# A mixture of experts written as one line of steps, with a fixed order on three engines and four pairs of split weights

## The chip, the cores and the metric

The kernel runs on one core of a Trainium2 chip. The metric is the device time of one execution in microseconds (us), the median of several. PE is TensorE, ACT is ScalarE, DVE is VectorE, POOL is GpSimd and SP is SyncE, whose queue issues most of the DMAs.

## The reference

One decoder layer in float32 on 1024 tokens of width 1024. Its last part, a mixture of experts, is what the change touches: each token goes to one of four groups and there to two of eight experts of inner width 512.

```python
x = x + parallel_mixer(rms_norm(x))          # window attention | spatial gating
x = x + memory_cross_attention(rms_norm(x))
# mixture of experts, for every token t and its two experts e:
hid = silu(x_t @ w1[e]) * (x_t @ w3[e])      # 1024 -> 512
y_t += gate[t, e] * (hid @ w2[e])            # 512 -> 1024
```

The experts' weights are 32 x 3 matrices of 1024 x 512 in float32, 2 MB each.

## The kernel before

The layer runs in stages: token mixer, memory attention, then the mixture of experts, which the change concerns. In it the program keeps 32 lists of up to 96 tokens (`cap`, `n`), one list for each expert, in the tile `idx`, and the experts are taken in a fixed line (`order`). For one expert the work is:

- GpSimd gathers its 96 rows from DRAM into X0 or X1 (L1027, two buffers in turn). TensorE transposes them in eight 128-wide pieces (L1044), and ScalarE and VectorE split the result into a high half xh and a remainder xl (L107, L108).
- SyncE brings the expert's weights as twelve tiles `ew` of 128 x 1024 (512 KB) into a ring of 36 tiles (`nraw` 19 and `nmore` 17). ScalarE casts each tile into `hi` (L1054), VectorE subtracts to get `lo` (L1055). A pair hi, lo lives in one of three pairs of buffers (`nhl` 3), and is released by the last of the six matmuls that read it. These six are two times the three products hi*xh, lo*xh and hi*xl (L115, L116, L117). The text calls such a group of a tile a step: eight steps go up, into two accumulators `h` of 96 x 512, and four go down, into two accumulators `y`.
- Between up and down lie silu on ScalarE (L1073), a product on VectorE (L1074, tile `g`), four transposes (L1081) and their split (hh, hlo).
- ScalarE multiplies y with the gate into the tile B (L1098, two instructions), and GpSimd adds B to the output in DRAM (L1033, "scatter"). B has one buffer.

`Moe.main` writes this expert by expert, with the down steps of the expert before behind the up steps of this one. Within that, the order of the instructions on each engine is chosen by the scheduler that builds the program. `rest` is the second half of the routing, with the gates of half of the tokens: twelve small products on GpSimd fill two tiles `vg` (L982, one buffer), four matmuls read each (L985), VectorE adds to `tb`, which holds the gates. `between` runs it after the first four up steps of expert 0. `counts` (L1159 to L1172) are eight matmuls, and on VectorE some twenty small instructions on 128 x 32 elements that depend on one another; they decide on a loop for lists that overflow, and stand at expert 20.

Of the kernel before, what the change touches and what calls it, by code (L numbers as in the profile page):

```python
# [17 lines left out]
P = 128  # L18
# [810 lines left out]
class Moe:  # L829
# [4 lines left out]
    def __init__(self, tc, a, L, m, cap):  # L834
        self.tc, self.nc, self.a, self.L, self.m = tc, tc.nc, a, L, m
        self.cap = cap

# [43 lines left out]
    def route(self, hf):  # L881
# [95 lines left out]
        n = 0  # L977
        for e in range(2):
            vg = w.tile([P, 2, 3, 4, NE], BF16, name="vg")
            for k in range(3):  # L980
                for i, x in enumerate((rb[:, k, e], rb[:, k, 2])):
                    G.tensor_tensor(vg[:, i, k], E[:, e], bc(x, NE), op=ALU.mult)  # L982
# [53 lines left out]

    def columns(self, x, n):
        nc, L, m = self.nc, self.L, self.m
        xh = L["ew"].tile([P, 8, self.cap], R32, name="xh", bufs=1)
        xl = L["ew"].tile([P, 8, self.cap], R32, name="xl", bufs=1)  # L1040
        for h in range(2):
            pt = L["ps"].tile([P, 4, P], F32, name="tp", bufs=2)
            for k in range(4):
                nc.tensor.transpose(pt[:, k, :n], x[:n, (4 * h + k) * P:(4 * h + k + 1) * P], m.ident[:n, :n])  # L1044
            s = slice(4 * h, 4 * h + 4)
            m.split(xh[:, s, :n], xl[:, s, :n], pt[:, :, :n])
        return xh, xl

    def parts(self, w):

        L, nc = self.L, self.nc
        hi = L["hl"].tile([P, 1024], R32, name="hi", bufs=self.nhl)
        lo = L["hl"].tile([P, 1024], R32, name="lo", bufs=self.nhl)
        nc.scalar.copy(hi, w)  # L1054
        nc.vector.tensor_sub(lo, w, hi.bitcast(F32))  # L1055
        return hi, lo

    def hidden(self, w, xc, rs, n, between=lambda: None):
# [3 lines left out]
        for i in range(2):  # L1062
            if i:
                between()
            p = L["ps"].tile([P, 512], F32, name="h", bufs=4)
            for u in range(4):
                wh, wl = self.parts(w[i][u])
                for j in range(2):
                    k, s = 2 * u + j, slice(j * 512, (j + 1) * 512)
                    m.mm3(p[:n], xh[:, k, :n], xl[:, k, :n], wh[:, s], wl[:, s], k == 0, k == 7)  # L1070
            ps.append(p)
        g = L["ew"].tile([P, 512], F32, name="g", bufs=1)
        nc.scalar.activation(g[:n], ps[0][:n], AF.Silu, scale=rs[:n])  # L1073
        nc.vector.scalar_tensor_tensor(g[:n], ps[1][:n], rs[:n], g[:n], op0=ALU.mult, op1=ALU.mult)  # L1074
        return g

    def turn(self, g, n):
        nc, L, m = self.nc, self.L, self.m
        pt = L["ps"].tile([P, 4, P], F32, name="tp", bufs=2)
        for k in range(4):  # L1080
            nc.tensor.transpose(pt[:, k, :n], g[:n, k * P:(k + 1) * P], m.ident[:n, :n])  # L1081
        hh = L["ew"].tile([P, 4, self.cap], R32, name="hh", bufs=1)
        hl = L["ew"].tile([P, 4, self.cap], R32, name="hlo", bufs=1)
        m.split(hh[:, :, :n], hl[:, :, :n], pt[:, :, :n])
        return hh, hl

    def output(self, w, hc, b, gate, n):
        nc, L, m = self.nc, self.L, self.m
        hh, hl = hc
        py = [L["ps"].tile([P, 512], F32, name="y", bufs=2) for _ in range(2)]  # L1090
        for k in range(4):
            wh, wl = self.parts(w[2][k])
            for h in range(2):
                s = slice(h * 512, (h + 1) * 512)
                m.mm3(py[h][:n], hh[:, k, :n], hl[:, k, :n], wh[:, s], wl[:, s], k == 0, k == 3)
        for h in range(2):
            s = slice(h * 512, (h + 1) * 512)
            nc.scalar.activation(b[:n, s], py[h][:n], AF.Copy, scale=gate[:n])  # L1098
# [4 lines left out]
    def main(self, xd, out, pre, rest):  # L1103
# [13 lines left out]
        X, B = (lambda i: self.X[i % len(self.X)]), (lambda i: self.B[i % len(self.B)])  # L1117
        get = lambda i: self.gather(X(i)[:n], ix(i), xd)
        for i in range(len(self.X)):
            get(i)  # L1120
        xc = self.columns(X(0), n)
        prev = None
        turned = []

        def between():
            run_all(rest)
            if prev:
                turned.append(self.turn(prev[3], n))

        def finish():  # L1130
            i, e, w, g = prev
            b = B(i)
            self.output(w, turned.pop() if turned else self.turn(g, n), b, tb[:, 0, e:e + 1], n)
            ordered(self.scatter(b[:n], ix(i), out), i)

        for i in range(NE):
            if i == 20:
                self.counts()
            e = order[i]
            w = pre.pop(e) if e in pre else self.expert(e)  # L1140
            if i + len(self.X) < NE:
                get(i + len(self.X))
            with self.tc.issue_after(self.ready.ins) if i == 0 else nullcontext():
                g = self.hidden(w, xc, tb[:, 1, e:e + 1], n, between)
            if i + 1 < NE:
                xc = self.columns(X(i + 1), n)
            if prev:
                finish()
# [279 lines left out]
```

## Time and profile before

| what | value |
|---|---|
| median of three runs | 1301.59 us (1296.95 to 1305.77) |
| the profiled execution | 1294.25 us |
| its span, first to last instruction | 1292.5 us |
| PE busy | 1225.0 us, 95% of the span |
| DVE busy | 983.0 us, 76% |
| ACT busy | 851.8 us, 66% |
| POOL busy | 195.1 us, 15% |

The span leaves 1.75 us of the profiled execution outside. That execution is 7.34 us below the median of the three, which themselves lie 8.82 us apart. Time is counted from the start of the span. The expert stage begins at 689.06 us with the first matmul of expert 0 and lasts to the end.

### The profile page before, as it was taken

The page shows a single profiled execution, that of the slowest core. Times are in us where ns is not written, and L with a number is a line of the kernel's source. Part 1 is how long each engine was busy: PE and PEld are TensorE (multiplying, and loading weights), DVE is VectorE, ACT ScalarE, POOL GpSimd, SP SyncE. Part 2 cuts the span into 40 slices and gives each one's busy share as a digit, 9 for nine tenths or more (in the row PEclk, how much of TensorE's full clock was granted, in tenths as well). Part 3 has the DMA queues.
Part 4 walks back from the last instruction along what each step waited for, and adds up shares of the span by engine and source line. Part 5 has one row for each costly group of instructions (what it writes and reads, how often), then busy time and mean ns, then how long its engine had stood idle before and what let it go on. Part 6 is the DMA issues. An engine that isn't in the chain of part 4 may idle for free.

```text
span 1292.5 us, 17753 instructions
## 1 busy us (share of the span) xinstructions
PE 1225.0 (95%) x5967; PEld 925.7 (72%) x5967; DVE 983.0 (76%) x1587; ACT 851.8 (66%) x1335; POOL 195.1 (15%) x229
## 2 busy tenths in 40 slices
PE   8999889999999999999978999999999999999995
PEld 6886668887887777888754777777777767666663
DVE  6558896556376998546567999999999999888884
ACT  6458663445357764445334888888888888877773
POOL 1311320011211113010013111111111111111000
PEclk9999899998999999999989999999999999999998
DMA  8527566345333346632799989999999999999921
GB/s 290 157 75 232 185 164 206 114 123 183 119 106 114 115 146 188 189 92 87 250 356 352 348 289 384 360 383 380 389 379 380 383 376 383 369 379 360 378 55 15
DMA packets 116190, 317.81 MB, mean 246 GB/s; under 512 B 13824, under 2 KB 35456, under 8 KB 116096
## 3 DMA queue, kind: packets, MB, share of 16 engines
q1 hardware_dynamic: 95280, 283.04, 60.5%
q0 software_dynamic: 12224, 29.38, 9.2%
q10 hardware_dynamic: 8592, 4.23, 1.1%
q8 instruction: 48, 0.79, 0.3%
q14 instruction: 46, 0.38, 0.1%
HBM read 293.52 MB, written 31.46 MB: 251 GB/s over the span
## 4 chain that ended last, share of the span: by engine, by line
issue 40%; PE 32%; DVE 8%; DMA 7%; POOL 7%; ACT 3%; POOLq 0%; SPq 0%; DVEq 0%; ACTq 0%
PE mm L115 7%; PE mm L117 7%; PE mm L116 7%; POOL out_dram L1033 3%; POOL X L1027 2%; DMA out_dram<-st 2%; DVE wlo L100 2%; DMA raw<-in_wp_dram 2%; DVE S L498 1%; PE sc L115 1%; DMA ew<-in_wm_dram 1%; PE sc L116 1%; PE sc L117 1%; DVE S L481 1%; ACT whi L99 1%
## 5 line engine op out<-in xcount | busy, mean ns | idle before, releaser
L1055 DVE TENSOR_TENSOR lo<-ew,hi 128x1024 fp32r<-128x1024 f32 x384 | 457.6, 1220 | 65.6 <-ACT hi L1054 55.4
L1054 ACT CAST hi<-ew 128x1024 fp32r<-128x1024 f32 x384 | 398.0, 1050 | 84.6 <-PE h L117 54.8
L116 PE MATMUL h<-lo,xh 128*96 128x512 f32 x512 | 204.8, 400 | 5.9 <-DVE lo L1055 5.9
L115 PE MATMUL h<-hi,xh 128*96 128x512 f32 x512 | 201.2, 395 | 3.4 <-ACT hi L1054 2.6
L117 PE MATMUL h<-hi,xl 128*96 128x512 f32 x512 | 202.1, 395 | 0.3 <-DVE xl L108 0.3
L115 PE MATMUL mm<-ah,whi 128*128 128x512 f32 x416 | 165.3, 399 | 4.4 <-ACT whi L99 2.6
L117 PE MATMUL mm<-ah,wlo 128*128 128x512 f32 x416 | 163.2, 393 | 1.5 <-DVE wlo L100 1.5
L99 ACT CAST whi<-raw 128x1024 fp32r<-128x1024 f32 x92 | 96.2, 1049 | 103.7 <-PE mm L116 56.5
L116 PE MATMUL mm<-al,whi 128*128 128x512 f32 x416 | 163.5, 393 | 0.0
L100 DVE TENSOR_TENSOR wlo<-raw,whi 128x1024 fp32r<-128x1024 f32 x92 | 112.0, 1224 | 54.8 <-ACT whi L99 54.8
L116 PEld LDWEIGHTS h<-lo,xh 128*96 128x96 f32 x512 | 82.7, 161 | 45.5 <-DVE lo L1055 10.2
L115 PEld LDWEIGHTS h<-hi,xh 128*96 128x96 f32 x512 | 82.6, 161 | 41.5 <-ACT hi L1054 5.6
L117 PEld LDWEIGHTS h<-hi,xl 128*96 128x96 f32 x512 | 82.7, 161 | 33.4 <-DVE xl L108 1.2
L116 PE MATMUL y<-lo,hh 128*96 128x512 f32 x256 | 102.2, 399 | 0.1
L117 PE MATMUL y<-hi,hlo 128*96 128x512 f32 x256 | 100.6, 393 | 0.0
L115 PE MATMUL y<-hi,hh 128*96 128x512 f32 x256 | 96.3, 400 | 0.9 <-ACT hh L107 0.9
L115 PE MATMUL mm<-whi,ah 128*128 128x512 f32 (+1 forms) x256 | 95.0, 371 | 0.2 <-DVE kn L280 0.2
L116 PE MATMUL mm<-wlo,ah 128*128 128x512 f32 (+1 forms) x256 | 93.6, 366 | 0.8 <-DVE wlo L100 0.8
L117 PE MATMUL mm<-whi,al 128*128 128x512 f32 (+1 forms) x256 | 93.6, 366 | 0.0
L115 PEld LDWEIGHTS mm<-ah,whi 128*128 128x128 f32 x416 | 78.3, 189 | 20.5 <-ACT whi L99 3.5
L117 PEld LDWEIGHTS mm<-ah,wlo 128*128 128x128 f32 x416 | 78.3, 188 | 19.0 <-DVE wlo L100 3.0
L116 PEld LDWEIGHTS mm<-al,whi 128*128 128x128 f32 x416 | 78.4, 188 | 15.3 <-DVE al L111 0.5
(318 smaller groups left out, 1976.6 us busy)
## 6 DMA issues: line engine op xcount, KB each, us to landing
ew<-in_wm_dram SPq DMA_DIRECT2D x384, 512.0 KB
raw<-in_wp_dram SPq DMA_DIRECT2D x92, 512.0 KB
xr<-in_xT_dram SPq DMA_DIRECT2D x24, 256.0 KB
xr<-in_x_dram SPq DMA_DIRECT2D x16, 256.0 KB
km<-md POOLq DMA_DIRECT2D x8, 512.0 KB, 4.5
x1d<-q SPq DMA_DIRECT2D x16, 256.0 KB
xr<-x1d SPq DMA_DIRECT2D x16, 256.0 KB
sq<-in_xT_dram SPq DMA_DIRECT2D x8, 256.0 KB
```

What stands on the lines that cost most here:

```text
L99: nc.scalar.copy(hi, w)
L100: nc.vector.tensor_sub(lo, w, hi.bitcast(F32))
L115: mm(out, ah, bh, start=start, stop=False)
L116: mm(out, ah, bl, start=False, stop=False)
L117: mm(out, al, bh, start=False, stop=stop)
L481: nc.vector.tensor_tensor_reduce(out=S[:, j, kc], in0=ps[:, i, kc], in1=self.mask[:, kc], scale=1.0, scalar=-3.0e38, op0=ALU.add, op1=ALU. ...
L498: nc.vector.tensor_scalar(S[:, j, kc], S[:, j, kc], st[:, 5, j:j + 1], None, op0=ALU.mult)
L1027: return self.nc.gpsimd.indirect_dma_start(out=x, out_offset=None, in_=src, in_offset=bass.IndirectOffsetOnAxis(ap=idx, axis=0), bounds_ch ...
L1033: return self.nc.gpsimd.indirect_dma_start(out=dst, out_offset=bass.IndirectOffsetOnAxis(ap=idx, axis=0), in_=x, in_offset=None, bounds_ch ...
L1054: nc.scalar.copy(hi, w)
L1055: nc.vector.tensor_sub(lo, w, hi.bitcast(F32))
```

## The change

The expert stage becomes one list of steps (eight up steps of expert i, four down steps of expert i-1, and so on). Every instruction of ScalarE, VectorE and TensorE for the experts is pinned to the order in which it is written (`self.pin`). A step's pair hi, lo is cut four steps ahead (`cut(s + lead)`, `lead` is `nhl`, now 4), for which the weight ring shrinks from 36 to 34 tiles. The eight transposes of X stand together, and the four of g. The two evictions of y are put behind two different casts. Both `vg` tiles are filled ahead of the gates' matmuls, and the gates' small math on VectorE stands ahead of the first up step. The third gather stands behind that filling. `counts` stands as one block in the first step of expert 20. The last expert uses a buffer X as its B, and accumulates y in `h`.

```diff
+    def split(self, hi, lo, src):
+        self.pin(self.nc.scalar.copy(hi, src))
+        self.pin(self.nc.vector.tensor_sub(lo, src, hi.bitcast(F32)))
+
+    def up(self, p, parts, xc, u, n):
+        (wh, wl), (xh, xl) = parts, xc
+        for j in range(2):
+            k, s = 2 * u + j, slice(j * 512, (j + 1) * 512)
+            self.mm3(p[:n], xh[:, k, :n], xl[:, k, :n], wh[:, s], wl[:, s], k == 0, k == 7)
...
         for e in range(2):
-            vg = w.tile([P, 2, 3, 4, NE], BF16, name="vg")
+            vg[e] = w.tile([P, 2, 3, 4, NE], BF16, name="vg", bufs=1 + hf)
...
+        if hf:
             yield
-            for t in range(4):
-                mm(pt, S[4 * e + t], vg[:, :, :, t], start=n == 0, stop=n == 7)
-                n += 1
+            gates(0)
+            gates(1)
...
-        for i in range(NE):
-            if i == 20:
-                self.counts()
-            e = order[i]
-            w = pre.pop(e) if e in pre else self.expert(e)
-            if i + len(self.X) < NE:
-                get(i + len(self.X))
-            with self.tc.issue_after(self.ready.ins) if i == 0 else nullcontext():
-                g = self.hidden(w, xc, tb[:, 1, e:e + 1], n, between)
-            if i + 1 < NE:
-                xc = self.columns(X(i + 1), n)
-            if prev:
-                finish()
-            prev = (i, e, w, g)
+        steps = []
+        for i in range(NE + 1):
+            steps += [(i, k, u) for k in range(2) for u in range(4) if i < NE]
+            steps += [(i - 1, 2, u) for u in range(4) if i]
...
+        def last(i):
+            self.weigh(B(i), Y.pop(i), gate(i), 1, n)
+            ordered(self.scatter(B(i)[:n], ix(i), out), i)
+
+        get(0)
+        get(1)
+        self.pinned(True)
+        cuts = {0: cut(0), 1: cut(1)}
+        next(rest)
+        cuts.update({s: cut(s) for s in range(2, lead)})
+        xc, xt = self.room(), take(0)
...
+        for s, (i, k, u) in enumerate(steps):
+            p = cuts.pop(s)
+            if k < 2:
+                if u == 0:
+                    H[i, k] = self.L["ps"].tile([P, 512], F32, name="h", bufs=4)
+                self.up(H[i, k], p, xc, u, n)
+            else:
+                if u == 0:
+                    Y[i] = self.sums("y" if i + 1 < NE else "h")
+                self.down(Y[i], p, hc, u, n)
+            if (k, u) == (0, 3) and i:
+                ht = self.turning(G.pop(i - 1), n)
+            elif (i, k, u) == (NE - 2, 2, 1):
+                ht = self.turning(G.pop(i + 1), n)
+            elif (k, u) == (1, 3) and i + 1 < NE:
+                xt = take(i + 1)
...
+            cuts[s + lead] = cut(s + lead)
+            if (i, k, u) == (0, 1, 0):
+                run_all(rest)
+            if k == 0 and u == 0 and i > 1:
+                last(i - 2)
+            if (k, u) == ((0, 3) if i else (1, 2)):
+                G[i] = self.gate(H.pop((i, 0)), norm(i), n)
+            if (k, u) == (1, 0) and i:
+                hc = self.turned(ht, n)
+            if (k, u) == (1, 3):
+                self.mult(G[i], H.pop((i, 1)), norm(i), n)
+            if k == 2 and u < 2 and i + 2 < NE:
+                xc = xc if u else self.room()
+                self.rows_turned(xc, xt, u, n)
+            if (k, u) == (2, 3):
+                self.weigh(B(i), Y[i], gate(i), 0, n)
+                if i + 2 > NE - 1:
+                    last(i)
...
+            if (i, k, u) == (20, 0, 0):
                 self.counts()
...
-        moe.turns, moe.nraw, moe.nmore, moe.nhl = 0, 19, 17, 3
+        moe.turns, moe.nraw, moe.nmore, moe.nhl = 0, 19, 15, 4
```

Three places show what moves. On ScalarE, an expert late in the line, before: `hi` is a cast of a weight tile, xh and hh are halves of transposed tiles, g is silu, B the eviction of y.

```order
L1073 ACTIVATE g<-h,tb 96x512
L1054 CAST hi<-ew 128x1024 x4
L107 CAST xh<-tp 128x384 x2
L1054 CAST hi<-ew 128x1024 x3
L1098 ACTIVATE B_6768<-y,tb 96x512 x2
L1054 CAST hi<-ew 128x1024 x2
L107 CAST hh<-tp 128x384
L1054 CAST hi<-ew 128x1024 x3
L1073 ACTIVATE g<-h,tb 96x512
```

And now, the same engine in the same stretch:

```order
L1052 CAST hh<-tp 128x384
L1052 CAST hi<-ew 128x1024 x4
L1052 CAST xh<-tp 128x384
L1052 CAST hi<-ew 128x1024
L1052 CAST xh<-tp 128x384
L1052 CAST hi<-ew 128x1024 x2
L1147 ACTIVATE B_6768<-y,tb 96x512
L1052 CAST hi<-ew 128x1024
L1147 ACTIVATE B_6768<-y,tb 96x512
L1052 CAST hi<-ew 128x1024 x3
L1113 ACTIVATE g<-h,tb 96x512
```

From one silu to the next there are twelve casts in both (now one of them is ahead of these rows, between silu and hh). The halves of X, which stood together, and the two evictions, which followed one another, now have casts between them, and hh stands right after silu's first cast.

On GpSimd at the first experts, before: X is gathered by L1027, and the twelve products fill `vg`.

```order
L945 TENSOR_SCALAR S<-i_413,keep 128x128 x2
L1027 DMA X_6766<-xd,idx 96x1024
L1027 DMA X_6767<-xd,idx 96x1024
L1027 DMA X_6766<-xd,idx 96x1024
L982 TENSOR_TENSOR vg<-E,rb 128x128 x12
L1027 DMA X_6767<-xd,idx 96x1024
L1027 DMA X_6766<-xd,idx 96x1024
```

And now:

```order
L950 TENSOR_SCALAR S<-i_413,keep 128x128 x2
L1040 DMA X_6766<-xd,idx 96x1024
L1040 DMA X_6767<-xd,idx 96x1024
L992 TENSOR_TENSOR vg<-E,rb 128x128 x12
L1040 DMA X_6766<-xd,idx 96x1024
```

The third gather, the second into the same X, has moved from ahead of the twelve products to behind them.

On VectorE at the counts, before: `lo` is the second half of a weight tile's split, `no` a step of the counts.

```order
L1161 COPY cnt<-tp 128x32
L1055 TENSOR_TENSOR lo<-ew,hi 128x1024
L1166 TENSOR_SCALAR no<-cnt 128x32
L1168 TENSOR_SCALAR no<-cnt 128x32
L1055 TENSOR_TENSOR lo<-ew,hi 128x1024
L1169 TENSOR_TENSOR no<-no 128x32
L1168 TENSOR_SCALAR no<-cnt 128x32
L1169 TENSOR_TENSOR no<-no 128x32
L1168 TENSOR_SCALAR no<-cnt 128x32
L1055 TENSOR_TENSOR lo<-ew,hi 128x1024
L1169 TENSOR_TENSOR no<-no 128x32
```

And now, the first rows of the block and what follows it, each part by itself:

```order
L1053 TENSOR_TENSOR lo<-ew,hi 128x1024 x2
L1274 COPY cnt<-tp 128x32
L1053 TENSOR_TENSOR lo<-ew,hi 128x1024
L1279 TENSOR_SCALAR no<-cnt 128x32
L1281 TENSOR_SCALAR no<-cnt 128x32
L1282 TENSOR_TENSOR no<-no 128x32
L1281 TENSOR_SCALAR no<-cnt 128x32
```

```order
L1282 TENSOR_TENSOR no<-no 128x32
L1283 TENSOR_REDUCE noc<-no 128x1
L1285 CAST noi<-noc 128x1
L1053 TENSOR_TENSOR lo<-ew,hi 128x1024 x4
L1053 TENSOR_TENSOR hlo<-tp,hh 128x384
```

Before, a `lo` stood behind every few steps of the counts; now all 21 steps behind the copy stand between two `lo`.

## Rows read from the trace of the kernel before

**Rows 1.** Windows of the span: busy us by engine, clock, DMA share, GB/s.

```profile
860.00:960.00 100.00, 100.00 (x476) 70.75 (x475) 91.12 (x91) 85.21 (x102) 14.86 (x12) 1.00 1.03 381
1130.00:1260.00 130.00, 121.99 (x558) 83.03 (x557) 107.20 (x108) 99.81 (x122) 15.36 (x12) 1.00 0.82 294
```

**Rows 2.** The chain that ended last, its scatters: start us, us, engine, row's tile.

```profile
725.33 1.52 POOL out_dram L1033
...
1045.68 1.44 POOL out_dram L1033
...
1064.57 1.44 POOL out_dram L1033
...
1252.84 1.41 POOL out_dram L1033
...
1278.92 1.14 POOL out_dram L1033
```

**Rows 3.** Timeline near 1044 and 1155 us: start us, us, engine, line, [idle before <-releaser].

```profile
1043.19 1.05 ACT L1054 CAST hi<-ew 128x1024 fp32r<-128x1024 f32 x1 [0.73 <-PE y L117]
...
1044.15 1.25 ACT L1098 ACTIVATE B<-y,tb 96x512 f32<-96x512 f32 x2
...
1153.63 1.26 ACT L1098 ACTIVATE B<-y,tb 96x512 f32<-96x512 f32 x2 [1.91 <-PE y L117]
...
1155.88 0.47 PE L115 MATMUL h<-hi,xh 128*96 128x512 f32 x1 [0.43 <-ACT hi L1054]
...
1157.14 0.47 PE L116 MATMUL h<-lo,xh 128*96 128x512 f32 x1 [0.79 <-DVE lo L1055]
```

**Rows 4.** The page's costliest groups: the two halves of a weight tile's split.

```profile
L1055 DVE TENSOR_TENSOR lo<-ew,hi 128x1024 fp32r<-128x1024 f32 x384 | 457.6, 1220 | 65.6 <-ACT hi L1054 55.4
L1054 ACT CAST hi<-ew 128x1024 fp32r<-128x1024 f32 x384 | 398.0, 1050 | 84.6 <-PE h L117 54.8
```

**Rows 5.** Timeline of PE, transposes and the matmuls behind them.

```profile
904.95 0.25 PE L1081 MATMUL tp<-ident,g 96*128 96x96 f32 x1
...
905.25 0.47 PE L116 MATMUL h<-lo,xh 128*96 128x512 f32 x1
...
913.42 0.66 PE L1044 MATMUL tp<-ident,X 96*128 96x96 f32 x6
...
913.86 0.46 PE L115 MATMUL y<-hi,hh 128*96 128x512 f32 x1
```

**Rows 6.** Timeline of PE, first expert.

```profile
689.06 0.47 PE L115 MATMUL h<-hi,xh 128*96 128x512 f32 x1 [0.24 <-ACT xh L107]
...
694.84 0.51 PE L985 MATMUL tp<-vg,S 128*128 128x192 bf16 x4
...
699.07 0.49 PE L985 MATMUL tp<-vg,S 128*128 128x192 bf16 x4 [2.80 <-POOL vg L982]
...
705.42 0.47 PE L115 MATMUL h<-hi,xh 128*96 128x512 f32 x1 [0.56 <-ACT xh L107]
```

**Rows 7.** Timeline of POOL and ACT, first expert.

```profile
690.08 3.41 POOL L982 TENSOR_TENSOR vg<-E,rb 128x128 bf16<-128x128 bf16 x6
...
695.49 3.54 POOL L982 TENSOR_TENSOR vg<-E,rb 128x128 bf16<-128x128 bf16 x6 [2.00 <-PE tp L985]
...
701.13 1.28 ACT L1073 ACT_TABLE_LOAD   x1
```

**Rows 8.** Timeline of DVE, two steps of the counts.

```profile
1045.42 0.19 DVE L1169 TENSOR_TENSOR no<-no 128x32 f32<-128x32 f32 x1
...
1045.64 0.25 DVE L1168 TENSOR_SCALAR no<-cnt 128x32 f32<-128x32 f32 x1
```

**Rows 9.** Timeline of PE, a wait in the last expert.

```profile
1271.81 0.47 PE L115 MATMUL y<-hi,hh 128*96 128x512 f32 x1 [0.94 <-ACT hh L107]
```

**Rows 10.** DMA queues, 760 to 1040 us: packets, MB, share of 16 engines.

```profile
q1 hardware_dynamic: 26878, 97.88, 90.0%
```

**Rows 11.** Timeline of SP's queue, the end of the weight stream.

```profile
1215.72 9.15 SPq L1004 DMA_DIRECT2D ew<-in_wm_dram  x7
```

More of the change, by code (lines that the diff above doesn't have):

```diff
@@ L1 @@
[L1 removed]
+from contextlib import ExitStack
 from itertools import chain, islice
@@ L1035, in scatter, with mm3, rows_turning @@
                                                  compute_op=ALU.add)
+    def split(self, hi, lo, src):
+        self.pin(self.nc.scalar.copy(hi, src))
+        self.pin(self.nc.vector.tensor_sub(lo, src, hi.bitcast(F32)))
+    def mm3(self, out, ah, al, bh, bl, start, stop):
+        mm, pin = self.nc.tensor.matmul, self.pin
+        pin(mm(out, ah, bh, start=start, stop=False))
+        pin(mm(out, ah, bl, start=False, stop=False))
+        pin(mm(out, al, bh, start=False, stop=stop))
+    def rows_turning(self, x, n):
+        pts = []
+        for h in range(2):
+            pt = self.L["ps"].tile([P, 4, P], F32, name="tp", bufs=2)
+            for k in range(4):
+                s = slice((4 * h + k) * P, (4 * h + k + 1) * P)
+                self.pin(self.nc.tensor.transpose(pt[:, k, :n], x[:n, s], self.m.ident[:n, :n]))
+            pts.append(pt)
+        return pts
@@ L1041, in columns @@
         for h in range(2):
[L1042 to L1047, printed above, removed]
-    def parts(self, w):
[L1051 to L1055, printed above, removed]
+            self.rows_turned(xc, pts, h, n)
@@ L1062, in hidden @@
         for i in range(2):
-            if i:
-                between()
             p = L["ps"].tile([P, 512], F32, name="h", bufs=4)
             for u in range(4):
[L1067 to L1070, printed above, removed]
+                self.up(p, self.parts(w[i][u]), xc, u, n)
             ps.append(p)
-        g = L["ew"].tile([P, 512], F32, name="g", bufs=1)
@@ L1085, in turn, with down @@
         return hh, hl
[L1087 to L1095, printed above, removed]
+    def down(self, py, parts, hc, k, n):
+        (wh, wl), (hh, hl) = parts, hc
@@ L1096, in output, with sums, weigh @@
         for h in range(2):
             s = slice(h * 512, (h + 1) * 512)
-            nc.scalar.activation(b[:n, s], py[h][:n], AF.Copy, scale=gate[:n])
+            self.mm3(py[h][:n], hh[:, k, :n], hl[:, k, :n], wh[:, s], wl[:, s], k == 0, k == 3)
+    def sums(self, name):
+        return [self.L["ps"].tile([P, 512], F32, name=name, bufs=4 if name == "h" else 2) for _ in range(2)]
+    def weigh(self, b, py, gate, h, n):
+        s = slice(h * 512, (h + 1) * 512)
+        self.pin(self.nc.scalar.activation(b[:n, s], py[h][:n], AF.Copy, scale=gate[:n]))
@@ L1100, in order, with output @@
+    def output(self, w, hc, b, gate, n):
+        py = self.sums("y")
+        for k in range(4):
+            self.down(py, self.parts(w[2][k]), hc, k, n)
+        for h in range(2):
+            self.weigh(b, py, gate, h, n)
     def order(self):
@@ L1115, in ordered @@
             touch.append((i, ins))
[L1117 to L1126, printed above, removed]
-            if prev:
[L1128 to L1134, printed above, removed]
@@ new lines, in main, with get @@
+        B = lambda i: self.B[0] if i + 1 < NE else X(i - 1)
+        gate = lambda i: tb[:, 0, order[i]:order[i] + 1]
+        norm = lambda i: tb[:, 1, order[i]:order[i] + 1]
+        steps = []
+        for i in range(NE + 1):
+            steps += [(i, k, u) for k in range(2) for u in range(4) if i < NE]
+            steps += [(i - 1, 2, u) for u in range(4) if i]
+        W, H, G, Y, lead = {}, {}, {}, {}, self.nhl
+        def get(i):
+            if i < NE:
+                self.gather(X(i)[:n], ix(i), xd)
@@ new lines, in cut, with take @@
+        def cut(s):
+            if s < len(steps):
+                i, k, u = steps[s]
+                if (k, u) == (0, 0):
+                    e = order[i]
+                    W[i] = pre.pop(e) if e in pre else self.expert(e)
+                return self.parts(W[i][k][u])
+        def take(i):
+            pts = self.rows_turning(X(i), n)
+            get(i + 2)
+            return pts
+        def last(i):
+            self.weigh(B(i), Y.pop(i), gate(i), 1, n)
+            ordered(self.scatter(B(i)[:n], ix(i), out), i)
```

66 lines of the change are left out of this document (51 added, 15 removed).

## The prediction

> **What bounds the kernel now.** I first read busy time by stretches. In the middle of the expert stage TensorE is busy 100.00 us of 100, with nothing waited for, and VectorE 91.12, ScalarE 85.21; late in it TensorE is busy only 121.99 of 130, at the same granted clock of 1.00 [rows 1]. So the stage is bound by TensorE's instructions for two thirds of its length, and by something else at its end. The chain of waits gives the size. Scatters of finished experts follow one another by (1045.68 - 725.33) / 18 = 17.80 us over the first 18 intervals; the next takes 18.89, and then ten take 1252.84 - 1064.57 = 188.27, where ten at 17.80 would be 178.0 [rows 2]. The timeline shows why. Near 1044 us a cast that waited for the end of y goes first on ScalarE and the two evictions of y behind it. Near 1154 us the evictions are first: ScalarE is idle 1.91 us until y ends, evicts for 1.26, and only then casts, and TensorE waits 0.43 for hi and 0.79 for lo [rows 3]. A cast takes 1.05 and a subtraction 1.22 [rows 4], 2.27 together. Matmuls follow at 0.231 us (between 905.25 and 913.42 there are 35, the first of them 0.31, 34 at 0.231) [rows 5], so a step of six takes 1.39. With three pairs, a pair that is released must be filled again two steps later, within 2.78: 0.51 to spare, less than an eviction of 1.26. The difference, 0.75, is close to the 0.79.
>
> **The change part by part.**
>
> *Four pairs and evictions behind casts.* A pair now has three steps, 4.16 us, for 2.27: 1.9 to spare. Ahead of the cast that is needed next stand at most one half eviction (0.63), or one half of xh, or hh, which are narrower (384 columns, not 512), and never two in a row. In one expert ScalarE has 85.21% of 17.80 = 15.2 us of work and VectorE 16.2 [rows 1], which the change doesn't raise; both stay below TensorE's 17.6. So I expect no wait from this place, and the late excess goes: 188.27 - 178.0 = **10.3 us**. Bounds: if half the waits stay, 5; it can't be more than 10.3.
>
> *Transposes.* 72 matmuls at 0.231 are 16.63, which leaves 1.17 of 17.80 for the twelve transposes. Before, they stand in three places. Three of them hold the matmuls up by 0.30 and six by 0.44 [rows 5]: about 0.05 each, and 0.16 for the interruption. Now there are two places (four and eight), so 0.15 an expert is saved, over 30 experts **4.5 us**. TensorE has nothing else to do there, so all of it lies on the path. Bounds: 0, if the interruption is no cost of its own, to 6.
>
> *Counts.* Two steps of the counts start 0.22 apart [rows 8]. Spread between lo's they cost one interval 18.89 - 17.80 = 1.09 [rows 2], which has the eight matmuls in it. Now 21 in one block are 21 * 0.22 = 4.6, and the lo behind them waits. 1.9 of that is covered by the four pairs, so TensorE waits 2.7, and the matmuls add 0.3, and what VectorE must make up after it some 0.4: 3.4 in place of 1.09, a **loss of 2.3 us**. Bounds: a gain of 0.5 (dependent steps at half that distance) to a loss of 5 (nothing covered).
>
> *The gates.* In expert 0 TensorE waits 2.80 us for the second `vg` [rows 6]: GpSimd could fill it only after the first was read, idle 2.00 and then 3.54 [rows 7]. With two buffers both are filled in a row, 3.41 + 3.54 = 6.95. If GpSimd begins no earlier than now, at 690.08 [rows 7], it ends at 697.0; the gates' matmuls stand behind five steps (30 * 0.231 = 6.9), at 696.6 with the delay of the next sentences. As VectorE's part of it now comes ahead of the up steps, I expect the start some 3 us sooner. So the 2.80 go, or all but 0.4. The third gather waits behind the filling, until 697 at the latest, but its rows are needed only when expert 1's up steps end, past 714. Against this, the gates' math on VectorE now stands ahead of some of the routing: about seven small operations of the kind in [rows 8], 1.5 us at the most, not all of them in its chain. I take 0.6 by which the first gather, and the first matmul, come later. At the end of expert 0 ScalarE has a cast, a load of tables (1.28) [rows 7], silu and xh in a row, and TensorE waited 0.56 for xh there [rows 6]; in the written order I expect 0.5 more. 2.80 - 0.6 - 0.5 = **1.7 us**. Bounds: -0.5 (1.5 late, and 1.8 for the chain) to 3.
>
> *The end.* From the 30th to the 32nd scatter there are 26.08 us [rows 2]. 96 matmuls (22.2) and two sets of transposes of g (0.33 each, 0.05 * 4 + 0.16) are 22.9: 3.2 are waits, one of them the 0.94 for hh [rows 9], which had nothing over it. Now the last g is turned between the second and third down step of the expert before, with 2.8 us of matmuls over it. The chain product, transposes, hh, hlo is still there, and I leave it 1.7: **1.5 us** gained. Bounds: 0 to 3.
>
> *Ring.* Two tiles fewer are two twelfths of an expert's time, 3 us of lead for the weights. Nothing shows it now: the last tile is issued at 1215.72 + 9.15 = 1224.87 [rows 11], 54 us before the last scatter. I cost it at nothing; what it could cost is the second rival.
>
> The sum is 10.3 + 4.5 - 2.3 + 1.7 + 1.5 = 15.7 us. The profiled execution of 1294.25 would become 1278.6. It lies 7.3 below the median, which I take for an offset that both kernels have: 1301.59 - 15.7 = **1286**.
>
> **Rivals.**
>
> *The line is slower everywhere.* This is the slower side. The scheduler's order reached 17.80 with three pairs over 18 intervals; a fixed order has each instruction wait for the one ahead of it, whatever is ready. If the place of one eviction or one half of xh is wrong, it is wrong in all 31 experts. The late cadence is the price: 18.83 a scatter, 1.03 more than 17.80. In all 30 intervals, it comes 18 to 20 times more than now, 1.03 * 18 = 18.5 lost, and the other terms (4.5 - 2.3 + 1.7 + 1.5 = 5.4) stand against it: about 1315. It decides from a wait of 0.5 us an expert (30 * 0.5 = 15). For it: VectorE is at 91% and has little room behind the product and xl, which come close together. Against: the pair to spare, 1.9 us, is three times the largest piece put between.
>
> *The weights become the bound.* From 760 to 1040 us the queue of the weights moved 97.88 MB [rows 10] in 280 us at a DMA share of 1.03 [rows 1]: 0.350 MB a us, and twelve tiles of 0.524 MB are 6.29 MB, so 18.0 us an expert. TensorE already takes them at 17.80 and lives on the lead that the ring built up; at 17.65 it uses up 0.35 an expert rather than 0.2. Over 20 experts that is 3 us more, and the ring's 3 us. If the lead is gone by expert 15, the other 10 or so go at 18.0: 10 * 0.35 + 3 = 6.5 back, 1292. Against it: the stream ends 54 us before the last scatter, and that moves to at least 35. Of this rival's size there is one more figure. The Trainium skill, on the page "DMA: Bandwidth & Descriptors", section "Where 436 GB/s comes from", says that for transfers from HBM to SBUF the HBM side binds, at about 358 GB/s. By that (an estimate) the 6.8 MB that an expert moves in 17.80 us at 381 would take 18.9, 29 intervals 548 us in place of 527.5, and the sum would be 1322. The trace disagrees, with 381 GB/s over 100 us [rows 1], so the rule gets no part of the chance.
>
> *The waits go, but little else.* Transposes in a row save nothing, the counts cost 5, and the beginning gains nothing: 10.3 - 5 + 1.5 = 6.8, so 1295. For it: nobody reads off a trace how transposes behave in a group of eight.
>
> **How the numbers follow.** What a measurement of this kernel can tell from no change is about 1%, 13 us. The forecast gets 0.63, the slower line 0.07, the weights 0.10, little else 0.20. 13 us faster is reached by the forecast if the counts and transposes aren't both at their worse bound: I put that at 0.56 of its 0.63, and 0.04 of the others. So faster 0.60, same 0.34, slower 0.06. The range: at the top 1299, with the weights and the third rival in it and 2 to 4 us for the medians; below, the better bounds of all terms are 10.3 + 6 + 0.5 + 3 + 3 = 22.8, of which not all will come together, so 1278. Left out above is nearly only the slower line.
>
> **What would show it.** Scatters 17.6 to 17.7 apart from the second to the last but one, and no waits of TensorE for hi or lo late in the stage; if they are 17.8, the transposes saved nothing. One longer interval at expert 20, by some 3 us, with a wait for lo behind the counts on VectorE. No wait for `vg`, the first matmul at about 689.7, and expert 1 at about 703.7. The forecast is wrong if TensorE waits in every expert for hi, lo or xl (the first rival), or for weights through ScalarE after expert 20 (the second).

## The result, and the profile after

The changed kernel takes 1285.3 us in the median of four runs (1284.14 to 1287.56), the kernel before 1301.49 (1296.95 to 1305.77). The ratio is 0.9878, with a 95% interval of 0.9842 to 0.9914: 1.2% faster, 16.2 us.

The windows of the profile after, with the columns of [rows 1], answer to those. Late in the stage TensorE is now as busy as in the middle of it, and the DMAs move no less than before (306 GB/s for 294):

```profile
860.00:960.00 100.00, 100.00 (x478) 71.24 (x477) 92.11 (x92) 85.42 (x103) 14.43 (x11) 1.00 1.03 378
1130.00:1260.00 130.00, 130.00 (x618) 92.48 (x617) 119.65 (x118) 111.42 (x133) 16.83 (x12) 1.00 0.84 306
```

The scatters of the chain answer to [rows 2]:

```profile
751.55 1.72 POOL out_dram L1046
...
1051.65 1.71 POOL out_dram L1046
...
1073.27 1.71 POOL out_dram L1046
...
1249.80 1.69 POOL out_dram L1046
...
1272.24 1.14 POOL out_dram L1046
```

From 751.55 to 1051.65 there are 17 intervals, 17.653 us each; then one of 21.62, and ten of 17.653 again. The late excess of 10.3 us is gone, the cadence is 0.15 below 17.80, and expert 20 costs 3.97 us where it cost 1.09. The list of all of TensorE's waits in the expert stage (line, what it waited for, us in total, times, longest) is short:

```profile
PE tp L1067 <- DMA X<-xd,idx: 4.6, 1, 4.6
PE h L1058 <- DVE lo L1053: 1.9, 1, 1.9
PE h L1057 <- ACT xh L1052: 1.5, 1, 1.5
PE h L1059 <- DVE xl L1053: 0.6, 1, 0.6
PE tp L1125 <- DVE g L1117: 0.3, 1, 0.3
```

Before, this list held 8.5 us of waits for lo and hi, and the 2.80 for vg [rows 6]. Behind the first two TensorE's clock is low for a while. On TensorE's timeline the wait for the first lo behind the counts is 1.88 us. Behind it nine matmuls start some 0.43 apart, and from 1061.59 on it is 0.23 again:

```profile
1057.86 0.60 PE L1058 MATMUL h<-lo,xh 128*96 128x512 f32 x1 [1.88 <-DVE lo L1053]
...
1058.26 0.63 PE L1059 MATMUL h<-hi,xl 128*96 128x512 f32 x1
...
1061.59 0.40 PE L1058 MATMUL h<-lo,xh 128*96 128x512 f32 x1
```

The window of that place shows the granted clock (the third number from the end) at 0.51, the lower of its two levels, where the windows above have 1.00:

```profile
1058.00:1061.00 3.00, 3.00 (x8) 1.94 (x9) 3.00 (x3) 0.79 (x1) 0.00 (x0) 0.51 0.98 370
```

The transposes stand as eight and four. The next matmul starts 0.60 us after the first of the eight, where six took 0.44 before [rows 5]:

```profile
865.29 0.82 PE L1067 MATMUL tp<-ident,X 96*128 96x96 f32 x8
...
865.89 0.45 PE L1057 MATMUL y<-hi,hh 128*96 128x512 f32 x1
```

The beginning answers to [rows 6] and [rows 7]. From the last msq on VectorE (L188), the same instruction in both kernels, it is 22.96 us to the first matmul of expert 0 and 38.27 to that of expert 1; before it was 19.34 and 35.70 (L188 stood at 669.72). There is no wait for vg, but one of 4.57 for the first gathered rows, which land 8.7 us after GpSimd begins to gather (6.2 before), and one of 1.45 for xh at expert 1:

```profile
674.13 0.16 DVE L188 TENSOR_SCALAR msq<-tp 128x4 f32<-128x4 f32 x1 [2.23 <-PE tp L198]
...
687.19 1.69 POOL L1040 DMA_INDIRECT X<-xd,idx  x1 [2.10 <-DVE lo L1053]
...
695.90 1.26 PE L1067 MATMUL tp<-ident,X 96*128 96x96 f32 x8 [4.57 <-DMA X<-xd,idx]
...
697.09 0.74 PE L1057 MATMUL h<-hi,xh 128*96 128x512 f32 x1
...
712.40 0.47 PE L1057 MATMUL h<-hi,xh 128*96 128x512 f32 x1 [1.45 <-ACT xh L1052]
```

The two profiled executions differ by only 6.7 us (1294.25 and 1287.56), since the first lies 7.2 below its median and the second 2.3 above. The last msq comes 4.4 us later in the second, in the stages that the change doesn't touch; counted from there, the changed kernel is 11.1 us faster, 13.7 of it from the first matmul of expert 1 to the last scatter, and -2.6 before.

### The profile page after: what moved, and what is told of

Read it like the earlier page. It is cut to its first block, busy times and chain, and to the rows that moved or that the text cites. A ratio compares the mean times of both kernels' runs of the same rounds, so it can differ in the third digit from the quotient of the medians.

```text
span 1285.8 us, 17703 instructions
## 1 busy us (share of the span) xinstructions
PE 1223.6 (95%) x5967; PEld 931.5 (72%) x5967; DVE 986.7 (77%) x1587; ACT 853.0 (66%) x1335; POOL 198.9 (15%) x229
## 5 line engine op out<-in xcount | busy, mean ns | idle before, releaser
L1053 DVE TENSOR_TENSOR lo<-ew,hi 128x1024 fp32r<-128x1024 f32 x384 | 462.8, 1223 | 47.2 <-ACT hi L1052 43.1
L1052 ACT CAST hi<-ew 128x1024 fp32r<-128x1024 f32 x384 | 402.8, 1049 | 88.4 <-PE y L1059 38.7
L1057 PE MATMUL h<-hi,xh 128*96 128x512 f32 x520 | 207.5, 399 | 1.6 <-ACT xh L1052 1.5
L1059 PE MATMUL h<-hi,xl 128*96 128x512 f32 x520 | 206.6, 397 | 0.6 <-DVE xl L1053 0.6
L1057 PE MATMUL y<-hi,hh 128*96 128x512 f32 x248 | 99.0, 399 | 0.0
L1059 PE MATMUL y<-hi,hlo 128*96 128x512 f32 x248 | 97.4, 393 | 0.0
L1058 PE MATMUL y<-lo,hh 128*96 128x512 f32 x248 | 97.3, 392 | 0.0
L1046 POOL DMA_INDIRECT out_dram<-B,idx x31 | 52.5, 1692 | 264.9 <-ACT B L1147 264.9
```

The costliest lines, as they stand in the source:

```text
L1046: return self.nc.gpsimd.indirect_dma_start(out=dst, out_offset=bass.IndirectOffsetOnAxis(ap=idx, axis=0), in_=x, in_offset=None, bounds_ch ...
L1052: self.pin(self.nc.scalar.copy(hi, src))
L1053: self.pin(self.nc.vector.tensor_sub(lo, src, hi.bitcast(F32)))
L1057: pin(mm(out, ah, bh, start=start, stop=False))
L1058: pin(mm(out, ah, bl, start=False, stop=False))
L1059: pin(mm(out, al, bh, start=False, stop=stop))
```

## Experiments

Counted on are mostly the traces: distances between scatters repeat to some 0.02 us, while medians of one kernel move by 1 to 3 us between sessions (the kernel before had 1301.49, 1299.02 and 1301.33).

### The late waits: pairs or order

**Three pairs in the written order.** The changed kernel with

```diff
-        moe.turns, moe.nraw, moe.nmore, moe.nhl = 0, 19, 15, 4
+        moe.turns, moe.nraw, moe.nmore, moe.nhl = 0, 19, 17, 3
```

> The changed kernel with three pairs hi, lo instead of four, and the ring at 36 tiles again; the written order stays. My theory is that the fourth pair is what gives the room (2.78 us instead of 4.16 between release and need, for 2.27 of work): with three, half an eviction (0.63) or half of xh between the casts is more than the 0.51 to spare, so TensorE waits some 0.1 to 0.5 us at two to four places of every expert. Scatters 18.2 to 19 us apart, the counts' block some 1.4 us worse: 1300 to 1325 us. The rival, that the order alone (a cast ahead of each eviction) takes the waits away, expects 17.65 to 17.75 throughout and only the counts' 1.4 more: 1287 us.

Measured: 1289.32 us (ratio 0.9922, 0.9892 to 0.9952). Its scatters:

```profile
1050.45 1.71 POOL out_dram L1046
...
1074.60 1.71 POOL out_dram L1046
...
1251.71 1.69 POOL out_dram L1046
```

Ten intervals of 17.71, and the counts 24.15. My theory fell: without the fourth pair there is no late wait either. The pair is worth 0.06 us an expert (a short wait for lo at one place, see the transposes below), and 2.5 us at the counts, whose block finds one step less cut ahead of it (TensorE's wait there is 3.28 instead of 1.88).

**Four pairs in the scheduler's order.** The kernel before with

```diff
-        moe.turns, moe.nraw, moe.nmore, moe.nhl = 0, 19, 17, 3
+        moe.turns, moe.nraw, moe.nmore, moe.nhl = 0, 19, 15, 4
```

> The kernel before with four pairs hi, lo and the ring at 34 tiles; nothing else of the change. If the pairs alone take the late waits away, scatters stay 17.80 us apart to the end, the 10.3 us of the late stretch go, and the time is about 1291 us. If the order is what matters, the scheduler's order still puts an eviction ahead of the cast that is needed next, TensorE still waits late, and the time is 1298 to 1302 us.

Measured: 1294.06 us (ratio 0.9965, 0.9944 to 0.9985). Its scatters, early and late:

```profile
729.87 1.52 POOL out_dram L1033
...
1047.62 1.44 POOL out_dram L1033
...
1175.30 1.44 POOL out_dram L1033
...
1233.97 1.43 POOL out_dram L1033
```

The first 18 intervals are 17.65, the last ones 19.56 (19.53 before). The late timeline shows the same two waits as [rows 3], though there is a pair more; ScalarE now idles 2.99 us ahead of the evictions where it idled 1.91:

```profile
1173.76 1.26 ACT L1098 ACTIVATE B<-y,tb 96x512 f32<-96x512 f32 x2 [2.99 <-PE y L117]
...
1176.01 0.48 PE L115 MATMUL h<-hi,xh 128*96 128x512 f32 x1 [0.44 <-ACT hi L1054]
...
1177.27 0.47 PE L116 MATMUL h<-lo,xh 128*96 128x512 f32 x1 [0.78 <-DVE lo L1055]
```

So the scheduler used the fourth pair to put the evictions still one cast earlier, and the late stretch gained next to nothing. From the first scatter to the last the trace gains 4.2 us: 2.6 by the early cadence (17.65 for 17.80, see the transposes below), 1.0 at the counts (17.93 for 18.89) and 0.6 in the ten intervals behind them. Neither of the two answers that I had written down fits: the time is between them, for a reason that was in neither.

**The written line without pins.**

```diff
-        self.pinned(True)
+        self.pinned(False)
```

> The changed kernel without the pins: the line is written in the same order, but the scheduler sets the order on ScalarE, VectorE and TensorE. In the order that it comes to, the evictions of the last seven or so experts stand two casts earlier than in the experts before them, as in the kernel before. My theory expects 17.65 to 17.7 up to about scatter 24, then 19.3 to 19.6 a scatter: 9 to 13 us more in the late stretch, 1292 to 1298 us. If the pins aren't what removes the late waits, scatters stay at 17.65 to the end and the time at about 1285.

Measured: 1292.46 us in one run. Up to the 23rd scatter they are 17.65 apart (17.93 at the counts), then 16.70, 17.51, 17.78, and four times 18.80:

```profile
1176.39 1.44 POOL out_dram L1046
...
1251.57 1.41 POOL out_dram L1046
```

From expert 1 to the last scatter it is 4.0 us longer than with pins, although the counts, which the scheduler spreads, cost it 3.7 less. The late cadence is lower than I had expected (18.80, not 19.3 to 19.6), but TensorE waits for lo late in the line again. The pins are what removes the late waits, not the form of the program.

**Evictions one cast earlier.** With all pins and four pairs, both evictions of y moved ahead of the casts that the last two down steps release. In the early experts of the kernel before they stand ahead of the cast of the last one, and "one cast earlier" counts from there. In the changed kernel they come later still: the first half moves by two casts here, the second by three.

```diff
-            cuts[s + lead] = cut(s + lead)
+            if k == 2 and u == 3 and i + 2 < NE:
+                self.weigh(B(i), Y[i], gate(i), 0, n)
+                last(i)
+                cuts[s - 1 + lead] = cut(s - 1 + lead)
+            if not (k == 2 and u == 2 and i + 2 < NE):
+                cuts[s + lead] = cut(s + lead)
...
-            if k == 0 and u == 0 and i > 1:
-                last(i - 2)
...
-            if (k, u) == (2, 3):
+            if (k, u) == (2, 3) and i + 2 >= NE:
                 self.weigh(B(i), Y[i], gate(i), 0, n)
-                if i + 2 > NE - 1:
-                    last(i)
+                last(i)
```

> The changed kernel, four pairs and pinned, with one edit in the line: both evictions of y stand one cast earlier on ScalarE, ahead of the casts that the last two down steps release (the place that the scheduler gives them late in the kernel before). My theory now is that this place alone makes the late cadence, whatever the number of pairs: at the end of y only two steps (2.78 us) are cut, and eviction 1.26, cast 1.05 and subtraction 1.23 take 3.54, so TensorE waits some 0.8 for lo and 0.4 for hi in every expert. Scatters 18.9 to 19.6 us apart over the whole line, 1322 to 1345 us. The rival, that four pairs cover it (1.9 to spare), expects 17.65 to 17.8 and no wait of TensorE: 1286 to 1290 us.

Measured: 1290.66 us in one run, scatters 17.84 apart, the counts 22.70:

```profile
745.69 1.45 POOL out_dram L1046
...
1049.08 1.44 POOL out_dram L1046
```

The cost is 0.19 an expert; this isn't the late cadence yet. I had taken two steps as cut at the end of y; but late in the kernel before only one is. From the end of y to the wait for hi at 1155.88 [rows 3] there are six matmuls of h, 0.23 apart:

```profile
1153.66 0.39 PE L117 MATMUL y<-hi,hlo 128*96 128x512 f32 x1
1153.89 0.39 PE L115 MATMUL h<-hi,xh 128*96 128x512 f32 x1
```

So one cast more:

```diff
-                cuts[s - 1 + lead] = cut(s - 1 + lead)
+                for r in (s - 2, s - 1):
+                    cuts[r + lead] = cut(r + lead)
-            if not (k == 2 and u == 2 and i + 2 < NE):
+            if not (k == 2 and u in (1, 2) and i + 2 < NE):
```

> As the run with the evictions one cast earlier, but two casts earlier: both evictions of y stand on ScalarE ahead of the casts that the last three down steps release, so that only one step (1.39 us) is cut when y ends. That is what the timeline of the kernel before shows late (six matmuls, then the wait for hi). One cast earlier cost 0.19 us an expert, since two steps are cut and y's first half ends 0.7 ahead of the second. My theory, that the late cadence comes from how early the eviction stands in ScalarE's line, expects now hi some 0.3 and lo 1.3 to 1.5 too late in every expert: scatters 19.0 to 19.6 us apart, 1322 to 1345 us. If this place isn't the cause, 17.8 to 18.2 and below 1305 us.

Measured: 1332.87 us in one run, scatters 19.24 apart all along the line (23.85 at the counts). The timeline of one expert is that of [rows 3] again, 0.32 for hi and 0.79 for lo, now with four pairs and in every expert:

```profile
861.38 1.38 ACT L1147 ACTIVATE B<-y,tb 96x512 f32<-96x512 f32 x2 [1.66 <-PE y L1059]
...
863.74 0.47 PE L1057 MATMUL h<-hi,xh 128*96 128x512 f32 x1 [0.32 <-ACT hi L1052]
...
865.00 0.47 PE L1058 MATMUL h<-lo,xh 128*96 128x512 f32 x1 [0.79 <-DVE lo L1053]
```

The matmul that waits for hi comes 0.48 later than 0.23 behind the one before it, the matmul that waits for lo 1.03, and the next 0.08: the 1.59 of an expert. That settles it: how early an eviction that waits for y stands in ScalarE's line makes the late cadence. Ahead of the casts of the last two down steps it costs 0.19 us an expert, ahead of those of the last three 1.59.

### The transposes

The changed kernel with the eight transposes of X in two groups of four, two steps apart:

```diff
+            elif (k, u) == (1, 1) and 0 < i and i + 1 < NE:
+                xt = take(i + 1, (0,))
             elif (k, u) == (1, 3) and i + 1 < NE:
-                xt = take(i + 1)
+                xt = (xt + take(i + 1, (1,))) if i else take(i + 1)
```

> The changed kernel with the eight transposes of X in two groups of four, two steps apart, so three groups an expert instead of two. My theory is that an interruption of the matmuls costs about 0.15 us by itself: scatters 17.78 to 17.82 us apart from expert 2 on, 4 to 5 us more in all. The rival, that the 0.15 us an expert came from something else (casts ahead of evictions, for one), expects 17.65 to 17.68 and no change.

Measured: 1281.0 us in one run, scatters 17.66 apart. Three groups cost what two cost. On the timeline four transposes hold the next matmul up by 0.28, and the one behind it comes 0.29 later instead of 0.23: 0.34 for four, 0.085 each, as 0.66 for eight in the kernel after:

```profile
855.88 0.49 PE L1067 MATMUL tp<-ident,X 96*128 96x96 f32 x4
...
856.16 0.45 PE L1057 MATMUL h<-hi,xh 128*96 128x512 f32 x1
```

So an interruption costs nothing by itself. In [rows 5] the odd one out is the first group, one transpose of g with two of X, 0.30 and 0.08 behind it: 0.38 for three, where three at 0.085 are 0.25. The third group of the same expert, three transposes of g, takes just that: the next matmul comes at 917.35, 0.19 behind the first of them, and the one behind it 0.06 late. The other 0.13 isn't a matter of transposes. The matmul behind the first group, at 905.25, reads the lo that VectorE began at 903.97, 1.28 us before. At the plain wait for lo in [rows 3] it is 1.28 as well, from 1155.86 to 1157.14:

```profile
903.97 3.50 DVE L1055 TENSOR_TENSOR lo<-ew,hi 128x1024 fp32r<-128x1024 f32 x3 [0.86 <-ACT hi L1054]
...
917.16 0.41 PE L1081 MATMUL tp<-ident,g 96*128 96x96 f32 x3
...
1155.86 2.36 DVE L1055 TENSOR_TENSOR lo<-ew,hi 128x1024 fp32r<-128x1024 f32 x2 [2.14 <-ACT hi L1054]
```

Up to 1030 us that trace has 18 such groups, and the distance is 1.28 or 1.29 in each. So most of the 0.15 an expert is a wait for lo, hidden behind three transposes: their rows reach beyond 905.25, so TensorE counts as busy and no wait is listed. With four pairs it is gone in the written order and in the scheduler's (17.65 in both). With three pairs in the written order a smaller one is left, with lo begun at 905.40 and read at 906.69, 0.07 late (17.71).

### The counts

The changed kernel with the 21 steps one to a step of the line:

```diff
             if (i, k, u) == (20, 0, 0):
-                self.counts()
+                spread = self.counts()
+            if i >= 20:
+                next(spread, None)
...
         for b in range(2 * self.cap, T, self.cap):
+            yield
             V.tensor_scalar(no[:, 1], self.cnt, float(b), None, op0=ALU.is_gt)
+            yield
             V.tensor_add(no[:, 0], no[:, 0], no[:, 1])
```

> The changed kernel with the 21 steps of the counts handed out one to a step of the line from expert 20 on, instead of in one block; same instructions. In the profile after, the block makes one interval 21.62 us long (17.65 else): 1.88 of it is TensorE's wait for lo, about 1.9 are ten matmuls at half the clock behind the wait. My theory is that both go: the longest interval 17.9 to 18.2, gain 3.4 to 3.9 us, about 1281.5 us. The rival, that VectorE has too little left over and the 4.6 us of steps come back as small waits later, expects intervals of 17.7 to 17.9 in the experts from 20 on and 1284 to 1285 us.

Measured: 1279.84 us (ratio 0.9843, 0.9809 to 0.9877). One interval of 17.94, and ten of 17.65 behind it:

```profile
1048.20 1.71 POOL out_dram L1046
...
1066.14 1.71 POOL out_dram L1046
...
1242.67 1.69 POOL out_dram L1046
```

From the first matmul of expert 1 to the last scatter it is 556.1 us, 3.7 less than the 559.8 of the changed kernel. VectorE has room for the steps (it is 92% busy), only not in one piece.

With three pairs and the ring of 36 (the edit of the first experiment) on top of it:

> The changed kernel with the counts spread one step at a time, and with three pairs and the ring of 36 tiles: what the fourth pair is worth when nothing long stands on VectorE. With three pairs and the counts in a block, scatters were 17.72 apart and the counts cost 6.4. If the fourth pair's worth is the 0.07 an expert alone, scatters are 17.72 apart, the longest 18.0 to 18.3, and the time is 2 to 3 us above the 1279.8 with four pairs: 1282 to 1283 us. If the pair was needed for the spread steps too, several intervals from expert 20 on are 18 to 19, and the time is 1285 or more.

Measured: 1283.6 us (ratio 0.9872, 0.9839 to 0.9904). Scatters are 17.72 apart, the longest 17.91, and from expert 1 to the last scatter it is 558.1, some 2 more than with four pairs. So without a block on VectorE the fourth pair is worth 2 us, and that has the two tiles in it that the ring gives up for it.

### The beginning

The gates as before, in expert 0 and with one buffer for vg:

```diff
-            vg[e] = w.tile([P, 2, 3, 4, NE], BF16, name="vg", bufs=1 + hf)
+            vg[e] = w.tile([P, 2, 3, 4, NE], BF16, name="vg")
...
-            if hf == 0:
-                yield
-                gates(e)
-        if hf:
             yield
-            gates(0)
-            gates(1)
+            gates(e)
...
-        next(rest)
```

> The changed kernel with the gates of the second half of the tokens as before: one buffer for vg, and their math in expert 0 instead of ahead of the first up step; all else is kept. From the last msq (L188) to the first matmul of expert 1 it was 35.70 us before and 38.27 after, where I had expected 34.0. If the gates' move is worth what I expected, its undoing brings a wait for vg of 2 to 3 us back and this distance becomes about 40, the time 1287 to 1288 us. The rival is that the move delays the first gather by more than it saves (first matmul of expert 0 at 22.96 us from msq after, 19.34 before): then its undoing brings that back to 19.5 to 20.5, and the distance to expert 1 is 36 to 38, the time 1283 to 1285. A third possibility is that the gather's landing (8.7 us from issue, 6.2 before) varies from execution to execution and belongs to neither.

Measured: 1288.91 us (ratio 0.9925, 0.9900 to 0.9949), from msq to expert 1 45.88 us, 7.6 more than in the profile after. The wait for vg is back, with 3.73:

```profile
707.73 0.80 PE L986 MATMUL tp<-vg,S 128*128 128x192 bf16 x4 [3.73 <-POOL vg L992]
...
716.82 0.47 PE L1052 MATMUL h<-hi,xh 128*96 128x512 f32 x1 [1.45 <-ACT xh L1047]
```

Behind it some ten matmuls start 0.43 apart, as they do behind the wait for the gather. In this execution the gates' move is worth more than I had put (45.88, where I had expected about 40), since it takes away a wait and what follows it. The rival fell: with the gates as before the first matmul comes 23.26 us from msq (694.20 less 670.94), no sooner than in the profile after (22.96). So the first matmul is as late without the gates' move.

The kernel before once more, for its profile:

> The kernel before, unchanged, for a second profile of its beginning. In the first one the first gather landed 6.2 us after GpSimd began it, in the profile after and three of its variants 7.6 to 9.7, and in the kernel before with four pairs 8.7. If the landing belongs to the execution and not to the kernel, this profile shows 7.5 to 9.5 and from the last msq to expert 1 some 38 to 40 us (35.70 in the first). If the changed beginning delays the gather, this shows 6 to 6.5 and 35.5 to 36.5 again. Scatters as in the first profile, 17.80 and late 19.5.

Measured: 1297.17 us in one run. The gather landed in 6.3 us, from msq to the first matmul it was 19.51, to expert 1 37.10. That is the second answer for the gather, not the first. Behind the same wait of 2.80 for vg as in [rows 6], seven matmuls start 0.43 apart, which they didn't in the first profile:

```profile
671.46 0.16 DVE L188 TENSOR_SCALAR msq<-tp 128x4 f32<-128x4 f32 x1 [1.87 <-PE tp L198]
...
690.97 0.47 PE L115 MATMUL h<-hi,xh 128*96 128x512 f32 x1 [0.24 <-ACT xh L107]
...
700.99 0.65 PE L985 MATMUL tp<-vg,S 128*128 128x192 bf16 x4 [2.80 <-POOL vg L982]
...
708.56 0.47 PE L115 MATMUL h<-hi,xh 128*96 128x512 f32 x1 [0.24 <-ACT xh L107]
```

But of ten profiles with the changed beginning or parts of it, two landed in 6.3 and 6.7 us (evictions one cast earlier, transposes in two), the others in 7.6 to 9.7, and the kernel before with four pairs in 8.7. In the two, the first matmul is 19.89 and 20.17 us from msq, 0.4 to 0.8 later than before, and expert 1 at 35.73 and 34.46. The first of these has some eight matmuls 0.43 apart behind the gather, the second has none. Like for like, 35.73 stands against 37.10 and 34.46 against 35.70: 1.2 to 1.4 us gained.

At last, with the counts spread, silu of expert 0 behind the split of expert 1's rows:

```diff
-            if (k, u) == ((0, 3) if i else (1, 2)):
+            if (k, u) == ((0, 3) if i else (1, 3)):
```

> The changed kernel with the counts spread, and with the silu of expert 0 behind the split of expert 1's rows on ScalarE instead of ahead of it. In every profile of the changed kernel TensorE waits 1.45 us there for xh, behind a load of tables (1.28) and silu (0.69). If that wait is only a matter of their place, it falls to 0 to 0.4, and from msq to expert 1 it is 1.0 to 2.0 us less for an equal landing of the gather; the time becomes about 1278.5 us. The rival is that the load and silu, 2.0 us together, now delay the casts behind them, and a wait for hi or lo of 0.5 to 1.5 takes its place in expert 1: no change, 1279 to 1280.

Measured: 1277.81 us (ratio 0.9826, 0.9789 to 0.9863), the lowest median of all these kernels; the 2.0 us to the 1279.84 with the spread counts alone are no more than medians move from session to session. The trace shows the effect by itself. The wait for xh at expert 1 is 0.24 instead of 1.45, and no other takes its place:

```profile
706.26 0.47 PE L1057 MATMUL h<-hi,xh 128*96 128x512 f32 x1 [0.24 <-ACT xh L1052]
```

From the first matmul of expert 0 to that of expert 1 it is 13.07 us, without a stretch at the lower clock. The pinned kernels with the gates moved took 14.3 (also without one) to 16.5.

## Why the prediction was right

The forecast of 1286 us is 0.7 above the median, and the sum holds from expert 1 on: 13.7 us gained in the trace, 14.0 by the four terms that belong there. But two of the terms had the right size for a wrong reason, and the 0.7 is in part luck. The sum took it that the profiled execution of both kernels lies 7.3 us below the median, and so expected 1278.6 for it; the profile after has 1287.56, 2.3 above its median. Counted from the last msq, the traces show 11.1 us gained, the medians 16.2.

- **The late excess.** 10.3 us, all of it gone, as forecast. The step that failed is its cause: "a pair now has three steps ... 1.9 to spare". The order does it, with three pairs as well; four pairs without the order leave it as it was. The agreement of 0.75 and 0.79 that I read from [rows 3] was an accident: I took two steps as cut when y ended, and it was one. What the rows do show, ScalarE idle 1.91 us with the eviction at the head of its line, was the cause; I named it and then reckoned with the number of pairs.
- **Transposes.** 0.15 us an expert, as forecast (17.65), but not from the transposes. The step "0.16 for the interruption" failed: a group costs some 0.083 to 0.085 a transpose (0.34 for four, 0.66 for eight), and 0.13 of the first group in [rows 5] was a wait for lo. With four pairs it is gone in either order. With three it is half as long in the written order (17.71). So this gain belongs to the order and the fourth pair, and "with nothing waited for", at the head of the prediction, isn't so.
- **Counts.** A loss of 2.9 us, with 2.3 forecast. The wait was 1.88, not 2.7; some 1.5 us more came from the lower clock behind it (21.62 with it, 20.07 without, last section), which the sum didn't have.
- **The gates.** The wait of 2.80 went, and the first matmul came 0.4 to 0.8 us later for a like landing (0.6 forecast). What failed is the size of the term in the profile after, -2.6 in place of +1.7: the gather landed 2.5 us later, and a wait of 4.57 for it is followed by six matmuls at the lower clock. With the fast landing, and like for like in the clock, the term is 1.2 to 1.4 (34.46 for 35.70, 35.73 for 37.10), with 1.7 forecast. Of its parts, the chain at the end of expert 0 was put too low: 0.9 more of a wait for xh (1.45 for 0.56), not 0.5. Whether the changed beginning makes the slow landing more likely stays open. Both profiles of before were fast, and two of ten others; but the kernel before with four pairs was slow (8.7), and so was, of the ten, the run with the gates as before (7.6).
- **The end.** By difference 1.9 us: 13.7 is 10.3, and 29 * 0.15 = 4.35, less 2.9, and the rest. 1.5 was forecast. That is what is left over and wasn't measured by itself; the wait of 0.94 for hh is no longer in the list.
- **The ring.** No cost that the trace shows: TensorE waits for no weights, and the last weight tile is issued at 1189.93 + 36.19 = 1226.1, 46 us ahead of the last scatter. "At least 35" stood in the second rival. On the Trainium skill's page "DMA: Bandwidth & Descriptors", section "Where 436 GB/s comes from", the HBM side binds such transfers at about 358 GB/s. The trace differs from that section after as before, with 378 GB/s over 100 us, and the 1322 us by it didn't come.

```profile
1189.93 36.19 SPq L1017 DMA_DIRECT2D ew<-in_wm_dram  x25
```

- **The rivals.** "Slower everywhere" needed an eviction in the wrong place, and its mechanism is real: ahead of the casts of the last three down steps it gave 1332.87 us. Its price was too low, 1.03 an expert and 1315 us. The ten late intervals in [rows 2] aren't one cadence: by the same chain three are 17.9, one is 18.69, one 18.26 and the last five 19.53, so the late place costs 1.73. The change has the eviction in the right place. "Little else" would have needed 17.80.

## What to carry to other kernels

ScalarE sat idle 1.91 us with an eviction at the head of its line and casts behind it. Where the order on an engine is fixed, an instruction that waits for another engine's result belongs behind everything that can be done before that result is there. Look for the instruction at the head of the line when the engine is idle and the bound engine starves a little later, and fix its place before adding buffers. A busy share of 100% can hide a short wait behind small instructions: compare the starts with those of a stretch that has none. A scheduler's order can drift along a loop: compare the last turns with the first ones. A block of small dependent steps on a busy engine can stall another one, so hand it out in pieces: the counts cost 3.97 us in one block and 0.29 one step at a time. With that and one silu moved, the kernel reaches 1277.81 us.

## What the runs showed of the hardware

I had not expected what a short wait can do to TensorE's clock. Behind the wait of 1.88 us at the counts the granted clock was 0.51 for about 3 us in the profile after, and 1.00 in that with the gates in expert 0, whose wait at the same place is as long. Its matmuls go on at once, and the interval is 20.07 in place of 21.62:

```profile
1062.29 0.48 PE L1053 MATMUL h<-lo,xh 128*96 128x512 f32 x1 [1.88 <-DVE lo L1048]
...
1062.60 0.40 PE L1054 MATMUL h<-hi,xl 128*96 128x512 f32 x1
```

Behind the 2.80 us for vg the kernel before had full speed in one execution and seven slow matmuls in the other. So such a wait can cost some 1.5 us on top of itself, and not in every kernel or execution. The Trainium skill, page "TensorE: Matmul & The Clock Gate", section "What's actually happening", says that a gate sets the clock by how busy the engine has been lately. The traces agree in that the low clock appears only behind waits in the expert stage of these runs, and show besides that a wait of one length may or may not bring it.
